# A two-layer hybrid attention and delta-rule backbone: high and low parts of queries, keys and values written by the stage that makes them, and loaded whole by the attention

## The chip, the cores and the metric

The kernel runs on one core of one Trainium2 chip. The metric is the device time of a run in microseconds (us). The profile covers one execution; its span goes from the first to the last instruction of the program, and a run's time is somewhat longer than the span.

The engines in the rows are PE (TensorE matmuls; PEld are its weight loads), DVE (VectorE), ACT (ScalarE), POOL (GpSimd) and SP (SyncE, which here issues all the transfers, in its own order; SPq is its sequencer). Each engine works through its instructions in the order in which they stand. Transfers run on the core's 16 DMA engines.

## The reference, cut to what matters

There are two layers over 1024 latent and 256 context tokens of width 1024. Each layer projects its input once, and the result goes to a latent attention (8 heads, 96 numbers per query and key, 64 per value) and to a gated delta rule (4 heads of 128). Both results go through one output projection, and a squared-relu MLP follows.

```python
p = h @ w_in
q_a, kv_a, k_r, qkv, z, a, b = jnp.split(p, _split_points(IN_SIZES), axis=-1)
q = (rmsnorm(q_a, q_a_g) @ w_q_b).reshape(B, T, MLA_HEADS, MLA_QK_DIM)
kv = (rmsnorm(kv_a, kv_a_g) @ w_kv_b).reshape(B, T, MLA_HEADS, MLA_NOPE_DIM + MLA_V_DIM)
q_nope, q_pe = q[..., :MLA_NOPE_DIM], q[..., MLA_NOPE_DIM:]
k_nope, v = kv[..., :MLA_NOPE_DIM], kv[..., MLA_NOPE_DIM:]
...
s = jnp.einsum('bqhd,bkhd->bhqk', qi, k).astype(jnp.float32) * scale
p = jax.nn.softmax(s, axis=-1).astype(v.dtype)
return jnp.einsum('bhqk,bkhd->bqhd', p, v)
```

All is float32. The kernel multiplies a pair of float32 matrices as three products of float32r parts: a value is its high part (a cast to float32r) plus a low part (the value minus the high part), and `mm3` adds high by high, high by low and low by high.

## The kernel before, in words

Tokens lie in three blocks: block 0 holds the 256 context tokens, blocks 1 and 2 hold 512 latent tokens each. The last layer has no queries in block 0. A layer has three stages.

Stage 1 (`stage1`) makes the input projection by tiles of 128 output columns (PE rows `mm`), the short convolutions, gates and chunk preparation of the delta rule, and the projections of the attention. `kv_proj` works block by block: four products of 128 output rows (`kps`, keys of two heads each, 64 numbers a head) and then one product for each 128 tokens (`vps`, values of all heads). `q_proj` makes four such products of queries (`qps`) and two more with the rotary columns of all heads. Each result is copied by ACT from its PSUM bank to a staging tile (`staged`, L720; tag `stg`, 3 buffers) and written to memory: keys to `kd` (L736, a transfer of 2 heads x 64 rows x 256 or 512 tokens), values to `vd` (L742, 128 tokens x 8 heads x 64), queries to `qd` (L766, again 2 x 64 x tokens) and rotary queries to `qd` (L779, 8 heads x 16 rows x tokens; in blocks 1 and 2 from a tile `rq` that shares the staging tiles' tag). Rotary keys follow in `kpe` (L601). The products' banks have the tag `pj`, with two buffers. So a product waits for a bank, a bank for its copy, and a copy for a staging tile whose write has landed.

Stage 2 runs attention and delta rule side by side. A unit of attention is 256 queries of one head (one per head for block 0, two for blocks 1 and 2). `front` makes the scores (`St` and `S` on PE), takes them out with their maximum (DVE, L878) and applies the exponential (ACT, L896). `back` transposes the results (`pt`), splits them into parts (`ph` on ACT, L927; `pl` on DVE, L928) and multiplies by the values (`o`). A head's keys, values and a block's queries come through `parts`: a transfer of at most 512 numbers per partition to a tile `raw` (L831, 3 buffers), an ACT cast to the high part (L832), and a subtraction for the low part (L834, on POOL except for the first heads, where it is on DVE). Key tiles alternate between two places by the head's parity, value tiles and query tiles have two buffers.

Stage 3 is output projection, norm and MLP.

The order on each engine is not written by hand. A scheduler places the instructions when the program is built, from its own estimate of their times. PE, ACT, DVE, POOL and SP then keep that order on the chip. Transfers take eight semaphores in turn, so that a transfer is issued only when the eighth before it has landed.

Of the kernel before, what the change touches and what calls it, by code (L numbers as in the profile page):

```python
# [17 lines left out]
P = 128  # L18
# [55 lines left out]
def host_layout(inp):  # L74
# [16 lines left out]
    # tiles of output columns: q 4, k 4, v 4, misc, kv_a, q_a 2, z 4  # L91
# [4 lines left out]
    # the rotary columns: first halves of all heads, second halves of all heads  # L96
# [19 lines left out]
class K:  # L116
# [13 lines left out]
    # ---------------------------------------------------------------- set-up  # L130
# [51 lines left out]
            # features and weights are queued behind the modulation's weights  # L182
# [93 lines left out]
    def ada_sum(self, l, v, m):  # L276
        """Eight columns that came by way of Pool and ACT, from their halves and the bias."""
        to = self.mod[l][v][:, m:m + 8]
        self.nc.vector.tensor_tensor(to, self.part[:, 0, v], self.part[:, 1, v], op=ALU.add)
        self.nc.vector.tensor_tensor(to, to, self.bada[l][:, m:m + 8], op=ALU.add)  # L280

    def load_sc(self, sp):
        """silu(c) and silu(c_ctx) on all partitions."""
        self.sc_b = []
        for v in range(2):
            t = sp.tile([P, D], F32, name=f"scr{v}")
            self.nc.sync.dma_start(t, self.scd[v].partition_broadcast(P))
            self.sc_b.append(t)

    def gain(self, l, j, vs):  # L290
        """(1 + scale) * gain of norm j."""
# [45 lines left out]
    def norm_mod(self, xs, rb, b, l, which, pool):  # L337
        """Modulated RMSNorm of block b (8 tiles [128, n]) into the high and low parts of h."""
# [22 lines left out]
    # ---------------------------------------------------------------- stage 1  # L361
    def stage1(self, l, last):
        """Input projection, short conv, gates, chunk preparation, latent attention's projections."""
# [8 lines left out]
        # the solves may go on into the next stage  # L372
# [16 lines left out]
        self.kd = dtile("kd", [H_A, DQK, NT])  # L389
        self.qd = dtile("qd", [H_A, DQK, NT])  # L390
        self.vd = dtile("vd", [H_A, P, NTT, 64])
# [40 lines left out]
        def conv_tile(m, blocks, it=None):  # L432
            """Projection, short conv, twice the silu."""
# [63 lines left out]
        lr = el.enter_context(self.pool(f"lr_{l}", side=self.osd))  # L497

        def first():
            """The first two output tiles, side by side, while the norm goes on."""  # L500
# [72 lines left out]
    def kpe(self, l, it, sp, tpp):  # L573
        """Rotary key part of all heads, and the gate columns by token."""
# [8 lines left out]
        for b, n, ps in it:  # L583
# [31 lines left out]
    def gates(self, l, stp):  # L615
        """Per-token scalars of both directions, [128 tokens, direction, tile, head]."""
# [45 lines left out]
        # the squares are of twice the features  # L662
# [24 lines left out]
    # ---- latent attention's low-rank parts  # L687
# [6 lines left out]
    def lowrank(self, raw, b, g, sp, stp):  # L694
        """RMSNorm of the low-rank features of block b, as high and low parts."""
# [21 lines left out]
    def staged(self, sp, src, n):  # L717
        t = sp.tile([P, 512], F32, tag="stg", name="stg", bufs=3)
        with self.hp_():
            self.nc.scalar.copy(t[:, :n], src)  # L720
        return t

    def kv_proj(self, l, raw, sp, mmp, stp):
        """Keys (but for the rotary part) and values of all heads, to DRAM as high and low parts."""
# [4 lines left out]
        for b, (t0, n) in enumerate(BLOCKS):  # L729
            xh, xl = self.lowrank(raw, b, g, sp, stp)[0]  # L730
            for m in range(4):
# [3 lines left out]
                t = self.staged(sp, ps[:, :n], n)  # L735
                nc.sync.dma_start(self.kd[2 * m:2 * m + 2, 0:64, t0:t0 + n], t[:, :n])  # L736
            for o in range(0, n, P):
# [3 lines left out]
                e = self.staged(sp, ps, 512)  # L741
                nc.sync.dma_start(self.vd[:, :, t, :].rearrange("h p c -> p h c"),  # L742
                                  e.rearrange("p (h c) -> p h c", c=64))

    def q_proj(self, l, raw, sp, mmp, stp):
# [3 lines left out]
        # the scale of the scores  # L749
        nc.vector.tensor_scalar(g, g, SM_SCALE, None, op0=ALU.mult)  # L750
        wk = [self.wload(io["w_qb"][l, :, k * QB:(k + 1) * QB]) for k in range(2)]
        for b in sorted({b for b, _ in raw}):
# [10 lines left out]
            for m in range(4):  # L763
                ps = qmm(m)
                t = self.staged(sp, ps[:, :n], n)
                nc.sync.dma_start(self.qd[2 * m:2 * m + 2, 0:64, t0:t0 + n], t[:, :n])  # L766
# [3 lines left out]
            for m in range(2):  # L770
                if b:
                    t = sp.tile([P, 512], F32, tag="stg", name="rq1", bufs=3)
# [4 lines left out]
                else:  # L777
                    t = self.staged(sp, ps[m][:, :n], n)
                nc.sync.dma_start(self.qd[:, 64 + 16 * m:80 + 16 * m, t0:t0 + n], t[:, :n])  # L779
# [10 lines left out]
        # the first scores wait for the products before them, not for the last transposes' banks  # L790
# [26 lines left out]
    def attention(self, l, last, ap, psA, psO):  # L817
# [4 lines left out]
        def parts(hi, lo, src):  # L822
            """Loads [p, n] or [p, t, n] values as their high and low parts."""
            p, m = src.shape[0], src.shape[1]
            w = 1 if len(src.shape) == 2 else src.shape[2]
            for c in range(0, m, 512 // w):
                e = min(m, c + 512 // w)
                raw = ap1.tile([P, 512], F32, tag="raw", name="raw", bufs=3)[:p, :(e - c) * w]
                if w > 1:
                    raw = raw.rearrange("p (t n) -> p t n", n=w)  # L830
                nc.sync.dma_start(raw, src[:, c:e])  # L831
                nc.scalar.copy(hi[:, c:e], raw)  # L832
                eng = nc.gpsimd if len(cur) > 3 else nc.vector
                eng.tensor_tensor(lo[:, c:e], raw, hi[:, c:e].bitcast(F32), op=ALU.subtract)  # L834

        def load(h):
            t = {}
            for nm in ("kh", "kl"):
                t[nm] = (ap2 if h % 2 else ap1).tile([DQK, NT], F32R, tag=nm, name=nm)
            parts(t["kh"], t["kl"], self.kd[h])  # L840
# [651 lines left out]
```

## Time and profile before

| | |
|---|---|
| median of 3 runs | 3953.94 us (3952.34 to 3956.1) |
| span of the profiled execution | 3929.9 us |
| difference of the two | 24.0 us |
| PE busy | 3517.4 us, 90% of the span |
| DVE, POOL, ACT busy | 2134.2, 1516.0 and 1459.3 us |
| moved by transfers | 372.52 MB, mean 95 GB/s |

No time of its own is given for the profiled execution beyond its span; the 24.0 us lie around the span and are taken as unchanged. Stage 2 lies at about 565 to 1075 us in layer 0 and 2620 to 3085 us in layer 1. The key, value and query projections of stage 1 lie at 105 to 264 us and at 2228 to 2378 us. A row of the stretches gives, for each engine, busy us and the number of its instructions, then PEclk (the granted share of TensorE's clock), the mean busy share of the 16 DMA engines, and what they moved. A wait is put down to what ended last before the waiting instruction. A time in brackets in a timeline is idle time before that instruction.

### The profile page before, as it was taken

What the parts mean: (1) busy time and instruction counts of PE and PEld (TensorE: products, weight loads), DVE (VectorE), ACT (ScalarE), POOL (GpSimd) and SP (SyncE); (2) the same over time, 40 slices, a digit from 0 to 9 for tenths busy, and PEclk for the clock granted to TensorE, in tenths of its full rate; (3) what the DMA queues carried; (4) which work ended last, traced back from release to release, by engine and by line L of the source; (5) the groups of instructions that cost most, each with busy time, mean ns of one, the idle gap of its engine ahead of it and who ended that gap; (6) DMA issues with size and microseconds to landing.
All of it is one profiled execution on the core that took longest, in us unless ns stands there. A gap on an engine that the chain in (4) does not pass through costs nothing.

```text
span 3929.9 us, 52618 instructions
## 1 busy us (share of the span) xinstructions
PE 3517.4 (90%) x19001; PEld 2992.1 (76%) x19001; DVE 2134.2 (54%) x4080; ACT 1459.3 (37%) x3156; POOL 1516.0 (39%) x1358
## 2 busy tenths in 40 slices
PE   8789977887887898999999978888889899999998
PEld 4668766787776777888888757767788788888887
DVE  5157855565769995333333627776667533333334
ACT  4334355565633111121112524336666531222122
POOL 3124864433354232232223313675533352333232
PEclk8899987898998899999999979989899899999999
DMA  5343465535353352111111334454653511111111
GB/s 186 91 136 116 139 149 94 112 93 95 77 199 102 129 180 81 43 44 38 38 33 43 102 94 132 144 147 109 125 101 81 132 57 46 52 51 49 44 54 54
DMA packets 335892, 372.52 MB, mean 95 GB/s; under 512 B 126849, under 2 KB 226577, under 8 KB 333969
## 3 DMA queue, kind: packets, MB, share of 16 engines
q1 hardware_dynamic: 335632, 369.18, 34.3%
q8 instruction: 149, 2.44, 0.3%
q14 instruction: 111, 0.90, 0.1%
HBM read 280.65 MB, written 88.42 MB: 94 GB/s over the span
## 4 chain that ended last, share of the span: by engine, by line
PE 57%; DVE 13%; DMA 12%; issue 5%; ACT 4%; POOL 3%; SPq 1%; POOLq 0%; DVEq 0%; ACTq 0%
PE f2ps L313 6%; PE f2ps L314 6%; PE f2ps L315 6%; PE fps L314 6%; PE fps L315 6%; PE fps L313 6%; DVE adaj L272 3%; DMA raw<-kd 3%; PE g L984 3%; PE o L916 3%; PE pt L924 2%; DVE cacc L444 2%; DVE A L1427 2%; DMA rinv<-rinv 2%; DMA adaw<-w_adaT 1%
## 5 line engine op out<-in xcount | busy, mean ns | idle before, releaser
L308 POOL TENSOR_TENSOR wlo<-wraw,whi 128x1024 fp32r<-128x1024 f32 (+1 forms) x190 | 462.3, 2441 | 1217.8 <-ACT whi L307 1217.8
L1304 DVE SCALAR_TENSOR_TENSOR x<-f2ps,mod,x 128x512 f32<-128x512 f32 (+1 forms) x648 | 440.9, 689 | 353.3 <-PE f2ps L315 353.1
L307 ACT CAST whi<-wraw 128x1024 fp32r<-128x1024 f32 (+1 forms) x190 | 195.6, 1046 | 1008.0 <-PE f2ps L314 692.7
L313 PE MATMUL f2ps<-ah,whi 128*128 128x512 f32 (+1 forms) x1296 | 474.4, 371 | 31.4 <-DVE x L1304 27.2
L314 PE MATMUL f2ps<-al,whi 128*128 128x512 f32 (+1 forms) x1296 | 478.5, 370 | 0.8 <-DVE al L1293 0.8
L313 PE MATMUL fps<-hh,whi 128*128 128x512 f32 (+1 forms) x1288 | 471.3, 368 | 8.8 <-ACT hh L351 8.8
L315 PE MATMUL f2ps<-ah,wlo 128*128 128x512 f32 (+1 forms) x1296 | 477.4, 369 | 0.0
L314 PE MATMUL fps<-hl,whi 128*128 128x512 f32 (+1 forms) x1288 | 474.1, 368 | 0.0
L315 PE MATMUL fps<-hh,wlo 128*128 128x512 f32 (+1 forms) x1288 | 472.9, 368 | 0.0
L1293 DVE TENSOR_TENSOR al<-relu,ah 128x256 fp32r<-128x256 f32 (+1 forms) x161 | 111.5, 699 | 512.9 <-POOL relu L1292 512.9
L313 PE MATMUL mm<-hh,whi 128*128 128x512 f32 (+1 forms) x880 | 333.1, 380 | 35.0 <-ACT craw L430 22.1
L314 PE MATMUL mm<-hl,whi 128*128 128x512 f32 (+1 forms) x880 | 331.4, 377 | 3.6 <-DVE hl L352 2.1
L315 PE MATMUL mm<-hh,wlo 128*128 128x512 f32 (+1 forms) x880 | 327.6, 374 | 0.8 <-POOL wlo L308 0.8
L928 DVE TENSOR_TENSOR pl<-pt,ph 128x512 fp32r<-128x512 f32 x328 | 222.2, 686 | 194.7 <-ACT ph L927 182.1
L313 PEld LDWEIGHTS f2ps<-ah,whi 128*128 128x128 f32 x1296 | 248.2, 192 | 74.4 <-DVE x L1304 29.9
L313 PEld LDWEIGHTS fps<-hh,whi 128*128 128x128 f32 x1288 | 243.7, 190 | 49.1 <-ACT hh L351 9.1
L314 PEld LDWEIGHTS f2ps<-al,whi 128*128 128x128 f32 x1296 | 248.7, 192 | 40.7 <-DVE al L1293 1.0
L315 PEld LDWEIGHTS f2ps<-ah,wlo 128*128 128x128 f32 x1296 | 248.4, 192 | 40.1
L314 PEld LDWEIGHTS fps<-hl,whi 128*128 128x128 f32 x1288 | 244.0, 189 | 40.1 <-POOL hl L357 0.3
L315 PEld LDWEIGHTS fps<-hh,wlo 128*128 128x128 f32 x1288 | 243.9, 189 | 39.8
L924 PE MATMUL pt<-ctab,p 128*128 128x128 f32 x1312 | 219.9, 287 | 32.9 <-ACT p L896 12.7
L1292 POOL TENSOR_TENSOR relu<-relu 128x256 f32<-128x256 f32 (+1 forms) x161 | 159.5, 996 | 225.2 <-ACT ah L1291 209.7
(287 smaller groups left out, 7520.6 us busy)
## 6 DMA issues: line engine op xcount, KB each, us to landing
wraw<-w_ff SPq DMA_DIRECT2D x128, 512.0 KB
adaw<-w_adaT SPq DMA_DIRECT2D x160, 256.0 KB
wraw<-w_in SPq DMA_DIRECT2D x40, 512.0 KB
QK<-QK SPq DMA_DIRECT2D x72, 256.0 KB
A<-A SPq DMA_DIRECT2D x40, 256.0 KB
v<-vtd SPq DMA_DIRECT2D x40, 256.0 KB
kt<-ktd SPq DMA_DIRECT2D x40, 256.0 KB
kT<-kTd SPq DMA_DIRECT2D x36, 256.0 KB
```

Source lines behind the costliest of these rows:

```text
L272: nc.vector.tensor_tensor_reduce(out=j, in0=w, in1=self.sc_b[v][:, s], op0=ALU.mult, op1=ALU.add, scale=1.0, scalar=acc if i else self.bad ...
L307: nc.scalar.copy(hi[:, :n], raw[:, :n])
L308: nc.gpsimd.tensor_tensor(lo[:, :n], raw[:, :n], hi[:, :n].bitcast(F32), op=ALU.subtract)
L313: then(mm(ps, lhsT=lh, rhs=rh, start=start, stop=False))
L314: then(mm(ps, lhsT=lh, rhs=rl, start=False, stop=False))
L315: then(mm(ps, lhsT=ll, rhs=rh, start=False, stop=stop))
L916: nc.tensor.matmul(o, lhsT=v[:, k, :], rhs=x[:, j, :], start=k == 0 and i == 0, stop=k == nkt - 1 and i == 1)
L924: self.mark = nc.tensor.transpose(tp[:, j, i * P:(i + 1) * P], pp[i][:, (k0 + j) * P:(k0 + j + 1) * P], self.ident)
L928: nc.vector.tensor_tensor(pl, tp, ph.bitcast(F32), op=ALU.subtract)
L984: nc.tensor.matmul(ps[:, h, :], lhsT=lhs[:, h, :], rhs=rhs[:, h, :], start=True, stop=True)
L1292: nc.gpsimd.tensor_tensor(r[:, :n], r[:, :n], r[:, :n], op=ALU.mult)
L1304: nc.vector.scalar_tensor_tensor(xs, ps[:, :n], g2, xs, op0=ALU.mult, op1=ALU.add)
```

## The change

Memory now holds both parts. `kd`, `qd` and `vd` have twice their size: keys and queries with an axis for the part, values with high and low part side by side (128 numbers a head and token). In stage 1 `staged` casts a product's bank to the high part on ACT and subtracts on DVE for the low part, and each key and query tile is written by two transfers, the value tile by one with both parts. The staging tiles are now four, of both parts each; three of them lie in space that the solves of the delta rule use later. `kpe` and the rotary queries are split in the same way. In stage 2 `parts` is gone: a head's keys are one transfer (96 x 2 x 1280), its values one (128 x 1280), a block's queries one (96 x 2 x tokens, now three buffers), straight into the operands of the products.

```diff
-        self.kd = dtile("kd", [H_A, DQK, NT])
-        self.qd = dtile("qd", [H_A, DQK, NT])
-        self.vd = dtile("vd", [H_A, P, NTT, 64])
+        self.kd = dtile("kd", [H_A, 2, DQK, NT])
+        self.qd = dtile("qd", [H_A, 2, DQK, NT])
+        self.vd = dtile("vd", [H_A, P, NTT, P])
...
+            parts = [sp.tile([P, 512], F32R, tag=nm, name=nm) for nm in ("gm", "gl")]
             for r, o in ((R1, 64), (R2, 80)):
-                nc.sync.dma_start(self.kd[:, o:o + 16, t0:t0 + n].rearrange("h r n -> r h n"),
-                                  kp[r, :n].unsqueeze(1).to_broadcast([16, H_A, n]))
+                nc.scalar.copy(parts[0][r, :n], kp[r, :n])
+                nc.gpsimd.tensor_tensor(parts[1][r, :n], kp[r, :n], parts[0][r, :n].bitcast(F32), op=ALU.subtract)
+                for i, x in enumerate(parts):
+                    nc.sync.dma_start(self.kd[:, i, o:o + 16, t0:t0 + n].rearrange("h r n -> r h n"),
+                                      x[r, :n].bitcast(F32).unsqueeze(1).to_broadcast([16, H_A, n]))
...
+    def staged(self, src, view):
+        t = self.stg[self.nstg % 4]
+        self.nstg += 1
+        hi, lo = view(t)
         with self.hp_():
-            self.nc.scalar.copy(t[:, :n], src)
-        return t
+            self.nc.scalar.copy(hi, src)
+            self.nc.vector.tensor_tensor(lo, src, hi.bitcast(F32), op=ALU.subtract)
+        return t.bitcast(F32)
...
-                t = self.staged(sp, ps[:, :n], n)
-                nc.sync.dma_start(self.kd[2 * m:2 * m + 2, 0:64, t0:t0 + n], t[:, :n])
+                t = self.staged(ps[:, :n], lambda t: (t[:, :n], t[:, 512:512 + n]))
+                for i in range(2):
+                    nc.sync.dma_start(self.kd[2 * m:2 * m + 2, i, 0:64, t0:t0 + n], t[:, i * 512:i * 512 + n])
...
-        def parts(hi, lo, src):
-                nc.sync.dma_start(raw, src[:, c:e])
-                nc.scalar.copy(hi[:, c:e], raw)
-                eng = nc.gpsimd if len(cur) > 3 else nc.vector
-                eng.tensor_tensor(lo[:, c:e], raw, hi[:, c:e].bitcast(F32), op=ALU.subtract)
...
         def load(h):
+            k = (ap2 if h % 2 else ap1).tile([DQK, 2, NT], F32R, tag="k", name="k")
+            nc.sync.dma_start(k.bitcast(F32), self.kd[h].rearrange("s r n -> r s n"))
+            v = ap2.tile([P, NTT, P], F32R, tag="v", name="v", bufs=2)
+            nc.sync.dma_start(v.bitcast(F32), self.vd[h])
+            cur[h] = k, v
```

SP in stage 1 of layer 0, from the first key write of block 0 to the last value write of block 2, before:

```order
L736 DMA kd_507<-stg 2x64x256 x2
L742 DMA vd_509<-stg 128x8x64 x2
L736 DMA kd_507<-stg 2x64x512 x3
L305 DMA wraw<-w_in 128x1024
L736 DMA kd_507<-stg 2x64x512
L742 DMA vd_509<-stg 128x8x64 x4
L736 DMA kd_507<-stg 2x64x512 x4
L742 DMA vd_509<-stg 128x8x64 x4
```

and the same place after (L755 writes keys, L765 values):

```order
L755 DMA kd_507<-stg 2x64x256 x4
L765 DMA vd_509<-stg 128x8x128 x2
L755 DMA kd_507<-stg 2x64x512 x4
L305 DMA wraw<-w_in 128x1024
L755 DMA kd_507<-stg 2x64x512 x4
L765 DMA vd_509<-stg 128x8x128 x4
L755 DMA kd_507<-stg 2x64x512 x8
```

Each key write stands twice, with the same shape of 2 x 64 x tokens, and the weight load (`wraw`) stands among them as it did.

ACT in stage 2 of layer 0, where the third head's keys come in, before (`kh`, `qh`, `v` are high parts that it casts from `raw`):

```order
L927 CAST ph<-pt 128x512
L832 CAST qh<-raw 96x512
L832 CAST kh<-raw 96x512
L896 ACTIVATE p,sm<-p,mn 128x256 x2
L1014 COPY U_4377<-B_4367 32x4x32 x4
L927 CAST ph<-pt 128x512
```

SP at the same head's keys, after (L857 loads queries, L849 keys):

```order
L857 DMA q<-qd_508 96x2x512
L849 DMA k<-kd_507 96x2x1280
L1011 DMA A_4444<-A_0_0_2670 64x4x64
L1011 DMA A_4444<-A_1_0_2673 64x4x64
L857 DMA q<-qd_508 96x2x256
```

The casts from `raw` between the attention's own ACT work are gone, and the third head's keys are issued right behind the queries of the second head's last block, while two units of that head are still to come.

## Rows read from the trace of the kernel before

**Rows 1.** Stretches: the projections (keys and values, then queries) of both layers.
```profile
105.00:175.00 70.00, 45.37 (x212) 36.30 (x211) 6.66 (x14) 18.68 (x37) 7.33 (x6) 0.76 0.30 86
175.00:264.00 89.00, 76.31 (x394) 64.64 (x395) 30.87 (x32) 29.81 (x87) 18.13 (x10) 0.92 0.33 100
2228.00:2298.00 70.00, 43.95 (x189) 32.36 (x189) 7.02 (x13) 21.47 (x57) 6.62 (x5) 0.79 0.37 101
2298.00:2378.00 80.00, 66.81 (x310) 55.95 (x311) 30.50 (x29) 23.29 (x56) 19.66 (x10) 0.87 0.31 98
```
**Rows 2.** Stretches: stage 2 of layer 0 and of layer 1.
```profile
565.00:1075.00 510.00, 410.45 (x2845) 373.10 (x2845) 314.89 (x916) 302.55 (x741) 207.54 (x258) 0.88 0.49 99
...
2620.00:3085.00 465.00, 409.09 (x2929) 371.11 (x2928) 313.96 (x907) 306.30 (x730) 209.49 (x286) 0.91 0.49 106
```
**Rows 3.** Timeline, ACT and then PE, key and value products of layer 1.
```profile
2282.11 0.59 ACT L720 COPY stg<-kps 128x512 f32<-128x512 f32 x1 [5.32 <-DMA kd<-stg]
...
2282.75 0.80 PE L313 MATMUL vps<-whi,nh 128*128 128x512 f32 x1 [4.93 <-ACT stg L720]
```
**Rows 4.** Narrow stretches with writes outstanding: keys 512 wide, queries 256 wide.
```profile
2278.00:2289.00 11.00, 2.50 (x5) 1.59 (x6) 0.00 (x0) 1.17 (x2) 0.00 (x0) 0.68 0.13 51
...
186.00:189.00 3.00, 3.00 (x18) 2.59 (x17) 0.00 (x0) 0.37 (x1) 0.00 (x0) 1.00 0.14 48
```
**Rows 5.** SP's timeline beside the first of them.
```profile
2274.12 9.92 SPq L736 DMA_DIRECT2D kd<-stg  x4
```
**Rows 6.** Transfers of the page by line: count and KB of one.
```profile
vd<-stg SPq DMA_DIRECT2D x20, 256.0 KB
...
kd<-stg SPq DMA_DIRECT2D x16, 256.0 KB
qd<-stg SPq DMA_DIRECT2D x16, 256.0 KB
...
qd<-rq SPq DMA_DIRECT2D x8, 256.0 KB
...
kd<-stg SPq DMA_DIRECT2D x8, 128.0 KB
...
qd<-stg SPq DMA_DIRECT2D x6, 128.0 KB
```
**Rows 7.** Narrow stretches: rotary query writes, value writes, 512-byte pieces of `kTd`.
```profile
216.00:218.00 2.00, 0.00 (x0) 0.00 (x0) 0.26 (x1) 0.58 (x2) 1.38 (x1) 1.00 0.75 242
2274.00:2275.00 1.00, 1.00 (x4) 0.81 (x3) 0.00 (x0) 0.10 (x1) 0.00 (x0) 0.50 1.08 256
221.50:223.50 2.00, 2.00 (x7) 1.52 (x6) 0.00 (x0) 2.00 (x14) 0.03 (x1) 0.50 0.96 298
```
**Rows 8.** Groups by line: a DVE subtraction that reads a PSUM bank.
```profile
L928 DVE TENSOR_TENSOR pl<-pt,ph 128x512 fp32r<-128x512 f32 x151 | 102.4, 686 | 98.9 <-ACT ph L927 95.3 <-PE o L916 2.4 <-issue 0.3
```
**Rows 9.** Waits in stage 2, layer 0 and then layer 1: total us, times, longest.
```profile
ACT kh L832 <- DMA raw<-kd: 83.5, 18, 10.1
...
ACT kh L832 <- DMA raw<-kd: 53.9, 12, 9.3
```
**Rows 10.** Timeline of layer 0, ACT and then PE, one wait for keys.
```profile
701.23 0.62 ACT L832 CAST kh<-raw 96x512 fp32r<-96x512 f32 x1 [4.52 <-DMA raw<-kd]
...
703.14 1.97 PE L1036 MATMUL g<-X,A 128*128 128x64 f32 x8 [4.21 <-ACT X L1029]
```
**Rows 11.** Chain that ended last, by line, stage 2 of layer 0, then layer 1.
```profile
by line: DMA raw<-kd 16.9%; DMA rinv<-rinv 10.3%; PE g L984 10.2%; PE o L916 8.8%; PE pt L924 6.9%; issue 5.2%; DMA B<-B 5.0%; PE S L313 3.4%; PE S L314 3.2%; PE S L315 3.2%; ACT p L896 2.3%; DMA rb<-rinv 2.0%; DVE p L878 1.9%; DMA raw<-vd 
...
by line: PE g L984 14.6%; PE o L916 13.9%; PE pt L924 11.4%; DMA raw<-kd 8.4%; PE S L313 5.2%; PE S L315 5.0%; PE S L314 4.9%; issue 2.8%; DMA wraw<-w_out 2.6%; DVE pl L928 1.8%; DMA raw<-vd 1.8%; DMA rinv<-rinv 1.8%; ACT ph L927 1.7%; DVE 
```
**Rows 12.** Work on `raw` in stage 2 of both layers: DVE, ACT, POOL busy.
```profile
565.00:1075.00 510.00, 0.00 (x0) 27.79 (x54) 55.87 (x54) 0.88 0.49 99
...
2620.00:3085.00 465.00, 0.00 (x0) 24.23 (x47) 51.41 (x48) 0.91 0.49 106
```

More of the change, by code (lines that the diff above doesn't have):

```diff
@@ L497, in stage1 @@
         lr = el.enter_context(self.pool(f"lr_{l}", side=self.osd))
+        self.open_stage(sv, lr)
         def first():
@@ L715, in lowrank, with open_stage @@
         return res
-    def staged(self, sp, src, n):
-        t = sp.tile([P, 512], F32, tag="stg", name="stg", bufs=3)
+    def open_stage(self, sv, sp):
+        both = sv.tile([P, 2048], F32R, tag="both", name="stg")
+        blb = sv.tile([P, 1024], F32R, tag="blb", name="stg")
+        own = sp.tile([P, 1024], F32R, name="stg")
+        self.stg = [both[:, :1024], both[:, 1024:], blb, own]
+        self.nstg = 0
+    def staged(self, src, view):
+        t = self.stg[self.nstg % 4]
+        self.nstg += 1
+        hi, lo = view(t)
         with self.hp_():
-            self.nc.scalar.copy(t[:, :n], src)
-        return t
+            self.nc.scalar.copy(hi, src)
+            self.nc.vector.tensor_tensor(lo, src, hi.bitcast(F32), op=ALU.subtract)
+        return t.bitcast(F32)
     def kv_proj(self, l, raw, sp, mmp, stp):
@@ L740, in kv_proj, with heads @@
                 self.mm3(ps, xh[:, o:o + P], xl[:, o:o + P], wh[:, 512:], wl[:, 512:], True, True)
-                e = self.staged(sp, ps, 512)
-                nc.sync.dma_start(self.vd[:, :, t, :].rearrange("h p c -> p h c"),
-                                  e.rearrange("p (h c) -> p h c", c=64))
+                def heads(t):
+                    e = t.rearrange("p (h c) -> p h c", c=P)
+                    return e[:, :, 0:64], e[:, :, 64:]
+                e = self.staged(ps.rearrange("p (h c) -> p h c", c=64), heads)
+                nc.sync.dma_start(self.vd[:, :, t, :].rearrange("h p c -> p h c"), e.rearrange("p (h c) -> p h c", c=P))
     def q_proj(self, l, raw, sp, mmp, stp):
@@ L764, in q_proj @@
                 ps = qmm(m)
-                t = self.staged(sp, ps[:, :n], n)
-                nc.sync.dma_start(self.qd[2 * m:2 * m + 2, 0:64, t0:t0 + n], t[:, :n])
+                t = self.staged(ps[:, :n], lambda t: (t[:, :n], t[:, 512:512 + n]))
+                for i in range(2):
+                    nc.sync.dma_start(self.qd[2 * m:2 * m + 2, i, 0:64, t0:t0 + n], t[:, i * 512:i * 512 + n])
             if b:
@@ L771, in q_proj @@
                 if b:
-                    t = sp.tile([P, 512], F32, tag="stg", name="rq1", bufs=3)
+                    t = sp.tile([P, 512], F32, tag="rq1", name="rq1", bufs=1)
                     q2 = sp.tile([P, 512], F32, tag="ls", name="rq2", bufs=2)
@@ L777, in q_proj @@
                 else:
-                    t = self.staged(sp, ps[m][:, :n], n)
-                nc.sync.dma_start(self.qd[:, 64 + 16 * m:80 + 16 * m, t0:t0 + n], t[:, :n])
+                    t = ps[m][:, :n]
+                x = self.staged(t[:, :n], lambda t: (t[:, :n], t[:, 512:512 + n]))
+                for i in range(2):
+                    nc.sync.dma_start(self.qd[:, i, 64 + 16 * m:80 + 16 * m, t0:t0 + n], x[:, i * 512:i * 512 + n])
     def stage2(self, l, last):
@@ L820, in attention @@
         cur = {}
-        def parts(hi, lo, src):
[L824 to L830, printed above, removed]
-                nc.sync.dma_start(raw, src[:, c:e])
-                nc.scalar.copy(hi[:, c:e], raw)
-                eng = nc.gpsimd if len(cur) > 3 else nc.vector
-                eng.tensor_tensor(lo[:, c:e], raw, hi[:, c:e].bitcast(F32), op=ALU.subtract)
-        def load(h):
[L837 to L840, printed above, removed]
-            t["v"] = v = ap2.tile([P, NTT, P], F32R, tag="v", name="v", bufs=2)
-            parts(v[:, :, 0:64], v[:, :, 64:], self.vd[h])
-            cur[h] = t
+        def load(h):
+            k = (ap2 if h % 2 else ap1).tile([DQK, 2, NT], F32R, tag="k", name="k")
[3 more added lines that the diff above has]
+            cur[h] = k, v
         def loadq(h, b):
             t0, n = BLOCKS[b]
-            cur[h, b] = r = [ap1.tile([DQK, 512], F32R, tag=nm, name=nm, bufs=2) for nm in ("qh", "ql")]
-            parts(r[0][:, :n], r[1][:, :n], self.qd[h, :, t0:t0 + n])
+            cur[h, b] = q = ap1.tile([DQK, 2, 512], F32R, tag="q", name="q", bufs=3)
+            nc.sync.dma_start(q[:, :, :n].bitcast(F32), self.qd[h, :, :, t0:t0 + n].rearrange("s r n -> r s n"))
         state = {}
@@ L861, in front @@
                 load(h)
-            t = cur[h]
-            qh, ql = cur[h, b]
+            kk, v = cur[h]
+            qq = cur[h, b]
             nk = NCTX if b == 0 else NT
@@ L871, in scores @@
                 q = slice(half * 256 + i * P, half * 256 + (i + 1) * P)
-                self.mm3(s, qh[:, q], ql[:, q], t["kh"][:, c0:c1], t["kl"][:, c0:c1], True, True)
+                self.mm3(s, qq[:, 0, q], qq[:, 1, q], kk[:, 0, c0:c1], kk[:, 1, c0:c1], True, True)
             pp = [ap.tile([P, NT], F32, tag="p", name="p", bufs=4) for _ in range(2)]
@@ L904, in front @@
             nc.sync.dma_start(rb[0:64], rd.rearrange("i p -> (i p)").partition_broadcast(64))
-            state[h, b, half] = (pp, rb, nk // P, t["v"])
+            state[h, b, half] = (pp, rb, nk // P, v)
         def back(h, b, half):
```

## The prediction

> **What bounds the kernel now.** I read the stretches first, to find where PE has room. PE is busy 90% of the span, so a change can win only where PE idles or where its clock is low. Two places of this change are such. In stage 2 PE is busy 410 of 510 us in layer 0 and 409 of 465 in layer 1, at a granted clock of 0.88 and 0.91 [rows 2]: 100 and 56 us idle. In the projections of stage 1 it is busy 45 of 70 us and 44 of 70 while keys and values are made, and 76 of 89 and 67 of 80 while queries are made [rows 1].
>
> Then I asked what ends the waits there. In stage 2 the reader is to see ACT stand before a cast of keys until `raw` has landed: 83.5 us in 18 waits in layer 0, 53.9 in 12 in layer 1 [rows 9]. ACT keeps its order, so everything behind the cast waits too, and PE with it: 4.52 us on ACT become 4.21 on PE a little later [rows 10]. The chain of work that ended last runs through these transfers for 16.9% of 510 us and 8.4% of 465, that is 86 and 39 us, and for 1.8% of 465 (8 us) through those of the values [rows 11].
>
> In stage 1 the wait is another one. ACT stands before a copy to a staging tile until an earlier key write has landed, 5.32 us for one, and PE then stands 4.93 us for ACT [rows 3]. Why a write takes so long is seen in the narrow stretch: four key writes are issued within 9.92 us [rows 5], and from 2278 to 2289 us, with nothing but these outstanding, the 16 DMA engines are busy to 0.13 and move 51 GB/s [rows 4]. 0.13 of 16 is two engines. A write of 2 heads x 64 rows goes through two engines, and the next one goes through the same two, otherwise the share would rise while several are outstanding. A 256 KB write thus costs 262144 B / 51 GB/s = 5.1 us of that pair, a 128 KB one 131072 / 48 = 2.7 us [rows 4]. The key phase is bound by this pair: per layer 8 x 5.1 + 4 x 2.7 = 52 us of its 70.
>
> **The change part by part.** The sum is made against the profiled execution: a span of 3929.9 us, and 24.0 us around it to the median of 3953.94.
>
> *Key and query writes, doubled.* Both layers have 16 + 8 key writes and 16 + 6 query writes from the staging tile [rows 6]; two of the six are rotary and are counted below. That is 32 of 256 KB and 12 of 128 KB: 32 x 5.1 + 12 x 2.7 = 196 us of the pair's time. After the change each stands twice with the same shape, so 196 us are added.
>
> *Rotary queries, doubled.* Ten more writes, eight of 256 KB [rows 6]. They move 242 GB/s, not 51 [rows 7], 1.1 us each: 10 us.
>
> *Value writes.* Twenty of 256 KB become twenty of 512 KB, in pieces of 512 bytes, not 256. At 256 bytes they move 256 GB/s, and other 512-byte pieces 298 [rows 7]: 1.76 - 1.02 = 0.74 us each, 15 us. The Trainium skill (DMA: Bandwidth & Descriptors, Specifications) speaks for this part: line rate needs pieces of at least 512 bytes, and shorter ones are read, modified and written. By it these bytes would be nearly free, and the sum 15 us smaller; the row, at 256 GB/s with short pieces, does not show such a loss, and I keep the 15.
>
> So 221 us of transfer time are added to phases of 309 us in all [rows 1]. How much room is there? In each phase the pair carries the narrow writes and a sixteenth of all else, which I estimate at 298 GB/s [rows 7]. Layer 0, keys: 86 GB/s x 70 us = 6.0 MB, less 2.6 MB narrow, 3.4 MB, 11 us; with 52 that is 63 of 70. In the same way 73 of 89 (layer 0, queries), 67 of 70 and 60 of 80. Free are 7 + 16 + 3 + 20 = 46 us. With all of it used the phases grow by 221 - 46 = 175 us; with none by 221. Below that, PE can run ahead of the pair by four staging tiles of 2 x 5.1 us, 41 us a layer, if its order holds enough other products and their weights are there: 175 - 82 = 93. I take 170, near the first value, because the weight loads stand in SP's order among the writes, as before, and so cannot run ahead.
>
> *The subtractions.* DVE gets one per staged tile, 24 for keys, 20 for values and 30 for queries, 0.69 us each as one that reads a bank [rows 8]: 51 us over both layers. The eight rotary tiles that POOL finished now pass ACT as well, 0.59 us each. DVE is busy 7 of 70 and 31 of 89 us there [rows 1], and the waits for the pair hide all of it. Without that cover each would hold a bank or a tile 0.7 to 1.3 us longer, 56 us at most.
>
> *Rotary keys.* Per block two casts and two subtractions more, on ACT and POOL, ahead of the writes. Nothing like it is in the trace; the nearest is one staged copy of 0.59 us [rows 3] plus 0.69 [rows 8], twice per block, 6 blocks: 15 us if all lies on the path, 0 if none. Their writes wait in SP's order with the weights behind them. I take 5.
>
> *Stage 2.* Gone are 52 us of ACT and 107 of POOL [rows 12], all beside PE's work and worth nothing by themselves, and the waits for `raw`. What is late next is the softmax chain: DVE waits 95.3 us for `ph` in layer 0 [rows 8], and a part of these waits is itself ACT standing at a cast. The gain cannot be more than what the chain spends in these transfers, 86 + 39 + 8 = 133 us, nor can it exceed the idle 156. It is not less than nothing by much: the bytes of the three loads double (about 10 MB a layer against 99 GB/s x 510 us = 50 MB [rows 2]) and delay the small transfers behind them, but they land directly. PE now waits for keys itself, and all of PE's order is queued behind that; yet the third head's keys are issued two units before their use. Two units of 40 in 510 us are 25 us, more than any wait of [rows 9], 10.1. I take 85, some two thirds of the chain's share, because the waits for `ph` and for the scores stay; ends 23 (half of the keys' 125 us stays, as waits of PE: 85 - 62) and 133.
>
> The sum: +170 + 5 - 85 = +90. 3929.9 + 90 = 4020 of span, **4044 us** with the 24 around it.
>
> **The rivals.** *A. The forecast:* the pair of engines decides, 4044.
>
> *B. Stage 2 wins, faster than before.* The mechanism is the backlog of staging tiles: PE's other products cover 41 us of writes in each layer, stage 1 costs 93, and the chain of stage 2 shortens by its whole 133. Time 3954 + 93 + 5 - 133 = 3919. It decides from the point at which the stretches of the projections grow by less than stage 2 shrinks. For it: PE is fully busy for the 3 us in which 256-wide writes are outstanding [rows 4], and its clock in stage 2 has 10% to regain [rows 2]. Against it: PE idles a third of the key phase already [rows 1], so the covering work is used up before.
>
> *C. The second part goes through other engines.* Then the pair carries no more than before, the rotary and value writes and the rotary keys cost 10 + 15 + 5 at most, and the time is 3954 + 30 - 85 = 3899. Against it: with several writes outstanding the share stays at 0.13 [rows 4, 5]. The Trainium skill (DMA: Bandwidth & Descriptors, Why a DMA increments its semaphore by 16 and not by 1) gives a rule that speaks against this change: a transfer takes the largest number of engines up to 16 that divides its slowest dimension larger than one, and the lowest-numbered ones. By that rule both parts, with 2 as that dimension, meet on one pair, and the trace agrees at 0.13 of 16; C is then out.
>
> *D. The change doesn't do what it says: stage 2 still waits, now on PE.* A head's keys are one transfer of 960 KB; the first scores need all of it, and SP's order can hold it back behind waits of others. With half of the keys' waits left the gain is 23, and the time 3954 + 170 + 5 - 23 = 4106. For it: the smaller transfers were late by up to 10.1 us [rows 9]. Against it: they were issued when a `raw` tile came free, and that reason is gone.
>
> **How the numbers follow.** Chances: A 0.68, B 0.10, C 0.04, D 0.18. A's own ends, 93 + 5 - 85 and 221 + 15 - 23, give +13 to +213, 3967 to 4167. Left out below 3955 are B and C (0.14), above 4135 the upper ends of A and D (0.06), where no room is used and little is gained; so the range is 3955 to 4135. A difference of 0.2%, 8 us, is about what a measurement of this kernel can tell from no change. Faster by more: B and C, 0.13. Within: 0.04, the edges of A and B. Slower by more: 0.83.
>
> **What would show it.** Stage 1 first: the stretch from the first key product to the last query product should take some 240 us in each layer, against 159 and 150 [rows 1], with long times at a DMA share of 0.13 and 51 GB/s, and ACT waiting for `kd<-stg` some 10 us at a time where it was 5 [rows 3]. If the share is 0.26 there, C is right. If these stretches grow by under 50 us a layer, the cover of B is there. In stage 2 the chain should hold no loads of keys, and PE's idle time should fall from 156 us to about 90; if PE waits for `k` or `q` for more than some 40 us in all, D is right. The forecast is wrong if the two-engine writes turn out to be hidden, or if stage 2 gives back more than 133 us, which only a regained clock could do.

## The result, and the profile after

The changed kernel takes 4131.98 us (median of 4 runs, 4126.7 to 4142.01), the kernel before 3953.14 us (4 runs, 3948.79 to 3956.1): a ratio of 1.0451, with a 95% interval of 1.0432 to 1.0471. It is 179 us slower. The prediction had 4044, and a range that ends at 4135, 3 us above the measured median.

The span and the busy times from the page of the changed kernel:

```profile
span 4140.2 us, 52501 instructions
...
PE 3522.0 (85%) x19001; PEld 2993.1 (72%) x19001; DVE 2161.8 (52%) x4140; ACT 1417.1 (34%) x3056; POOL 1421.3 (34%) x1264
```

PE does the same products in nearly the same time (3517 us before, 3522 after) and idles 618 us where it idled 412. Where it does is seen in the stretches. For each layer I cut the trace at PE's own instructions: the first key product, the last query product, the first scores (the start of stage 2) and the first output product after stage 2. The rows of before, cut like this (they take the place of [rows 1, 2], whose cuts were read by eye), layer 0 and then layer 1; columns as there, duration, busy us of PE, PEld, DVE, ACT and POOL, granted clock, DMA share, GB/s:

```profile
106.50:247.50 141.00, 111.46 (x548) 92.03 (x548) 34.08 (x41) 44.57 (x118) 19.24 (x12) 0.85 0.32 95
247.50:512.60 265.10, 239.95 (x1290) 201.93 (x1290) 199.36 (x217) 96.25 (x256) 173.26 (x133) 0.95 0.46 136
512.60:1098.80 586.20, 462.56 (x3177) 417.42 (x3176) 351.54 (x1021) 347.63 (x843) 245.91 (x322) 0.87 0.50 102
...
2226.60:2355.10 128.50, 99.19 (x449) 78.61 (x449) 27.34 (x35) 41.96 (x108) 18.63 (x11) 0.84 0.34 97
2355.10:2612.30 257.20, 226.03 (x1132) 185.54 (x1132) 193.94 (x217) 93.76 (x249) 159.89 (x121) 0.95 0.45 134
2612.30:3117.60 505.30, 428.27 (x3010) 385.81 (x3009) 330.71 (x936) 322.36 (x756) 232.07 (x307) 0.90 0.50 107
```

The same six of the changed kernel:

```profile
104.60:331.70 227.10, 128.70 (x605) 104.24 (x605) 63.57 (x85) 48.51 (x124) 21.45 (x13) 0.74 0.30 94
331.70:638.60 306.90, 236.23 (x1234) 197.20 (x1233) 189.39 (x208) 96.07 (x251) 181.08 (x148) 0.88 0.47 131
638.60:1199.20 560.60, 450.17 (x3178) 407.02 (x3177) 345.97 (x1020) 322.75 (x788) 186.11 (x259) 0.89 0.58 123
2323.50:2515.70 192.20, 108.45 (x449) 84.36 (x449) 45.70 (x68) 43.24 (x110) 18.61 (x11) 0.72 0.30 98
2515.70:2798.70 283.00, 227.65 (x1133) 185.74 (x1132) 195.21 (x213) 95.67 (x250) 169.10 (x132) 0.92 0.49 138
2798.70:3327.40 528.70, 423.41 (x3010) 384.03 (x3009) 332.36 (x937) 300.79 (x709) 179.35 (x255) 0.88 0.62 121
```

The projections grow by 86 and 64 us. The rest of stage 1, between the last query product and the first scores, grows by 42 and 26; stage 1 as a whole grows by 217. Stage 2 shrinks by 26 in layer 0 and grows by 23 in layer 1. Everything else together is 5 us shorter: 217 - 2 - 5 = 210 between the two spans. The medians differ by 179, because the profiled execution of before was a quick one (a span of 3929.9 us, where seven runs beside the experiments with the writes and the row sums have 3945.8 to 3960.9, each about 2 us under its time) and that of the changed kernel the slowest of its four. Single stretches therefore carry some 20 us of spread.

**Stage 1: the pair of engines, and SP behind it.** The stretch that answers to [rows 4], in which SP issues nothing but two-engine writes until 210 us, then ACT's timeline, SP's and DVE's in and beside it:

```profile
184.00:214.00 30.00, 4.40 (x10) 2.15 (x9) 1.50 (x4) 1.82 (x4) 0.00 (x0) 0.55 0.13 51
```

```profile
197.96 0.59 ACT L737 CAST stg<-vps 128x512 fp32r<-128x512 f32 x1 [14.60 <-DMA kd<-stg]
```

```profile
180.25 29.98 SPq L755 DMA_DIRECT2D kd<-stg  x7
```

```profile
183.39 0.69 DVE L738 TENSOR_TENSOR stg<-kps,stg 128x512 fp32r<-128x512 f32 x1 [0.59 <-ACT stg L737]
```

DMA share and rate are the 0.13 and 51 GB/s of [rows 4], now for 30 us on end, in which PE works 4.4. ACT's wait for an earlier key write is 14.60 us where [rows 3] had 5.32. New is the third row: SP needs 29.98 us to issue seven writes, 4.3 us each, near the 5.1 that the pair needs by the prediction to carry one. It does not stand for data: the last part of these key tiles is made by 184.1 us (fourth row). The list of instructions on the key tensor shows the same (count, then shortest, median and longest issue in ns; the first row is of the kernel before, the second of the changed one):

```profile
L736 SPq DMA_DIRECT2D kd<-stg x24: 478/498/2362, 107.5 to 2282.7; - x24
```

```profile
L755 SPq DMA_DIRECT2D kd<-stg x48: 492/2817/7162, 105.6 to 2430.0; - x48
```

While the pair is behind, issuing itself takes a median of 2.8 us instead of 0.5, and what stands between these writes in SP's order is issued late: the value writes, which spread over the engines [rows 7], take a median of 3.3 us to issue instead of 0.45. That is why the part after the projections grew too. SP's timeline at the last query product of layer 0, the waits from 320 to 420 us (total, times, longest), and the first 28.3 us behind that product as a stretch:

```profile
332.65 11.05 SPq L789 DMA_DIRECT2D qd<-stg  x3
343.80 4.91 SPq L305 DMA_DIRECT2D wraw<-w_in  x1
```

```profile
ACT whi L307 <- DMA wraw<-w_in: 26.2, 1, 26.2
PE tp L474 <- DVE cacc L451: 25.8, 1, 25.8
```

```profile
331.70:360.00 28.30, 3.15 (x14) 2.25 (x12) 2.05 (x4) 2.10 (x4) 0.00 (x0) 0.60 0.25 83
```

A load of weights is issued only at 343.8 us, behind the query writes, and takes 4.9 us to issue. ACT stands 26.2 us until it has landed, the rest of ACT's order stands behind that, and PE is busy for 3 of 28 us; in the kernel before PE was busy for 20.5 of the 28.3 us behind its last query product. Layer 1 has the same wait at its last query product, 35.4 us.

**Stage 2: the waits for keys are gone, the time is not.** No engine that computes has a wait that is put down to `k` or `q` (SP has, 4.0 us at the longest, and layer 1's chain has three pieces of them, 18 us together); the casts on ACT and their waits of [rows 9] don't exist any more. In their place stand waits for the reciprocal row sums, which in both kernels go to memory and come back to all partitions (`rinv` written, `rb` read). SP's and POOL's waits for them, of the changed kernel, layer 0 and then layer 1:

```profile
SPq L913 <- DMA rinv<-rinv: 197.3, 30, 13.1
...
POOL ob L950 <- DMA rb<-rinv: 78.5, 10, 15.5
...
SPq L913 <- DMA rinv<-rinv: 199.4, 27, 13.2
...
POOL ob L950 <- DMA rb<-rinv: 117.8, 14, 16.2
```

The same waits in the kernel before, layer 0 and then layer 1:

```profile
SPq L904 <- DMA rinv<-rinv: 137.9, 25, 8.3
...
POOL ob L941 <- DMA rb<-rinv: 16.6, 4, 6.3
...
SPq L904 <- DMA rinv<-rinv: 139.5, 23, 9.1
...
POOL ob L941 <- DMA rb<-rinv: 7.8, 2, 6.8
```

SP stands before the read back until the write has landed, for 277 us of stage 2 before and 397 after. The chain of layer 1 holds the same write for 16.0% where [rows 11] had 1.8% (of the changed kernel the chain does not reach back to layer 0):

```profile
by line: DMA rinv<-rinv 16.0%; PE g L993 9.9%; PE o L925 8.0%; PE pt L933 6.3%; DMA B<-B 5.8%; issue 4.3%; PE S L313 2.9%; PE S L315 2.7%; PE S L314 2.6%; DVE U L1025 2.6%; DMA craw<-catg 2.5%; DMA wraw<-w_out 2.2%; DMA rb<-rinv 2.2%; DMA q
```

### The profile page after: what moved, and what is told of

It is laid out like the page before. It is cut to its first block, busy times and chain, and to the rows that moved or that the text cites. A ratio compares the mean times of both kernels' runs of the same rounds, so it can differ in the third digit from the quotient of the medians.

```text
span 4140.2 us, 52501 instructions
## 1 busy us (share of the span) xinstructions
PE 3522.0 (85%) x19001; PEld 2993.1 (72%) x19001; DVE 2161.8 (52%) x4140; ACT 1417.1 (34%) x3056; POOL 1421.3 (34%) x1264
## 5 line engine op out<-in xcount | busy, mean ns | idle before, releaser
L313 PEld LDWEIGHTS mm<-hh,whi 128*128 128x128 f32 x880 | 175.3, 199 | 96.8 <-ACT craw L431 51.2
```

Source lines behind the costliest of these rows:

```text
L313: then(mm(ps, lhsT=lh, rhs=rh, start=start, stop=False))
```

## The experiments

The theory after the two traces: stage 1 is set by the pair and by SP standing behind it; stage 2 by the round trip of the row sums. The rivals: in stage 1 the subtractions, casts and bytes; in stage 2 the doubled loads. Two edits take away one suspect each, in both kernels.

**Writes by head (`w_after`, `w_before`).** The diff in the changed kernel, for keys; queries likewise, and the kernel before without the part dimension:

```diff
-for i in range(2):
-    nc.sync.dma_start(self.kd[2 * m:2 * m + 2, i, 0:64, t0:t0 + n], t[:, i * 512:i * 512 + n])
+for j in range(2):
+    nc.sync.dma_start(self.kd[2 * m + j, :, 0:64, t0:t0 + n].rearrange("s r n -> r s n"),
+                      t.rearrange("p (s c) -> p s c", s=2)[64 * j:64 * j + 64, :, :n])
```

> Each staged key or query tile of the changed kernel is written by head (two transfers of 64 rows x 2 parts x n) in place of by part (two of 2 heads x 64 rows x n): same bytes, same number of transfers. Theory (two engines carry all the narrow writes and set the length of the projections): with a write spread over the engines the stretch from first key product to last query product falls from 227 and 192 us to 120 or below in both layers, the DMA share of 0.13 with 51 GB/s is gone, and the time is some 3860 (3820 to 3950), below the kernel before. Rival (the added subtractions and casts, or the doubled bytes, are what costs): the stretches stay above 190 us and the time above 4050.

> The kernel before, each staged key or query write split into its two heads (64 rows x n each), so that the rows and not the heads are the outermost dimension; same bytes, twice the number of these transfers. Theory (the pair of engines already binds the projections before the change): the stretches of 141 and 128 us fall to 110 and 100, the time to some 3893 (3870 to 3920). Rival (PE's own work sets these stretches before, the pair only the changed kernel's): within 10 us of 3953.

**Row sums without memory (`r_after`, `r_before`).** The same in both kernels; `r` holds the reciprocal sums of 2 x 128 queries, one column each:

```diff
-rd = self.dr.tile([2, P], F32, name=f"rinv{l}_{h}_{b}_{half}")
-nc.sync.dma_start(rd.rearrange("i p -> p i"), r)
-rb = ap2.tile([P, 256], F32, tag="rb", name="rb", bufs=1)
-nc.sync.dma_start(rb[0:64], rd.rearrange("i p -> (i p)").partition_broadcast(64))
...
-nc.gpsimd.tensor_tensor(ob[0:64], ob[0:64], rb[0:64], op=ALU.mult)
+rb = psA.tile([P, 512], F32, tag="a", name="rbp")
+for i in range(2):
+    nc.tensor.matmul(rb[0:64, i * P:(i + 1) * P], lhsT=r[:, i:i + 1].to_broadcast([P, 64]), rhs=self.ident,
+                     start=True, stop=True)
+nc.vector.tensor_tensor(ob[0:64], ob[0:64], rb[0:64, :256], op=ALU.mult)
```

> The changed kernel, the reciprocal row sums no longer written to memory and read back to all partitions, but spread by two small matrix products (128 x 64 ones pattern, 128 columns) into a bank, with the last product on DVE in place of POOL. Theory (in stage 2 these round trips through memory, late under the doubled loads, have taken the place of the waits for the raw keys): stage 2 falls from 561 and 529 us by some 40 each, the time to some 4040 (4010 to 4070). Rival (the doubled loads slow stage 2 in another way, through the keys and queries that PE waits for): less than 30 us gained.

> The kernel before, with the same replacement of the round trip of the reciprocal row sums. Theory (before the change the loads of keys set stage 2 and the round trips a smaller part, some 60 us of the chain in layer 0 and 8 in layer 1): 20 to 60 us faster, some 3913. Rival (the round trips are covered by other work and matter in neither kernel): within 10 us of 3953.

Times beside 3953.85 us of the kernel before (7 runs), with the stretches of each profile, both layers added (projections; from there to the first scores; stage 2). The two kernels with both edits, which come next, stand here too, beside 3954.07 (7 runs):

| kernel | us | ratio to before, 95% | projections | to scores | stage 2 |
|---|---|---|---|---|---|
| before | 3953.14 | 1 | 270 | 522 | 1091 |
| after | 4131.98 | 1.0432 to 1.0471 | 419 | 590 | 1089 |
| `w_before` | 3869.43 | 0.9764 to 0.9806 | 203 | 510 | 1113 |
| `w_after` | 3888.54 | 0.9807 to 0.9869 | 230 | 532 | 1080 |
| `r_before` | 3795.87 | 0.9576 to 0.9618 | 271 | 527 | 952 |
| `r_after` | 3977.48 | 1.0039 to 1.0076 | 425 | 585 | 925 |
| `wr_before` | 3703.96 | 0.9355 to 0.9383 | 201 | 509 | 956 |
| `wr_after` | 3736.10 | 0.9436 to 0.9464 | 233 | 531 | 933 |

The writes by head take 243 us off the changed kernel and 84 off the kernel before, and 179 us between the two become 19. The theory's 3860 (up to 3950) holds for the changed kernel, though its layer 0 stays at 124 us, not 120 or below; the 3893 (3870 to 3920) for the kernel before was just too high. Both rivals, above 4050 and within 10 us of 3953, are out. Layer 0 of `w_after`, projections, and the issue of its key writes:

```profile
106.40:230.20 123.80, 114.00 (x605) 94.45 (x605) 64.58 (x85) 48.50 (x124) 21.02 (x13) 0.97 0.68 194
```

```profile
L755 SPq DMA_DIRECT2D kd<-stg x48: 574/612/1712, 107.9 to 2243.0; - x48
```

As many transfers of the same bytes, at a DMA share of 0.68 instead of 0.30, a granted clock of 0.97 instead of 0.74, and an issue of 0.61 us instead of 2.82. The order of the rows decided, not the number of transfers or bytes. By the Trainium skill (DMA: Bandwidth & Descriptors, Why a DMA increments its semaphore by 16 and not by 1) the outermost dimension, 64 rows here instead of 2 heads, divides among 16 engines instead of two; the trace agrees, with a share of 0.68 in place of 0.30.

The row sums take 154 us off the changed kernel (I expected 90) and 158 off the kernel before, where I expected 40. That the round trip binds both kernels alike, I had not seen. Waits of ACT for the raw keys in `r_before`, layer 0 and then layer 1:

```profile
ACT kh L832 <- DMA raw<-kd: 4.8, 5, 2.5
...
ACT kh L832 <- DMA raw<-kd: 14.3, 10, 4.2
```

In the stretches cut as above these were 83.5 and 56.5 us before. The loads of keys are untouched here, in the same pieces, into the same tiles, through the same casts, and 140 us of waiting for them have become 19. The waits which the prediction laid to the loads go with the round trip. By which way they go isn't shown: the edit ends SP's stand and also takes the last product off POOL, which in the kernel before stood idle ahead of that product for 107 and 41 us and which also makes the low parts that free the `raw` tiles. The stretch of stage 2, layer 0, `r_before` and then `r_after`:

```profile
513.20:1010.40 497.20, 462.37 (x3338) 404.79 (x3337) 371.45 (x1060) 348.79 (x844) 219.06 (x284) 0.98 0.41 115
```

```profile
640.90:1125.20 484.30, 461.82 (x3337) 405.49 (x3336) 361.73 (x1059) 322.33 (x786) 156.47 (x215) 0.98 0.49 136
```

PE is nearly the bound in both, 35 and 22 us idle, where it idled 124 and 110 with the round trip; 13 us are what direct loads save in this layer.

**Both edits (`wr_before`, `wr_after`), and who waits for the round trip (`q_before`).** `q_before` changes one word in two lines:

```diff
-nc.sync.dma_start(rd.rearrange("i p -> p i"), r)
+nc.gpsimd.dma_start(rd.rearrange("i p -> p i"), r)
...
-nc.sync.dma_start(rb[0:64], rd.rearrange("i p -> (i p)").partition_broadcast(64))
+nc.gpsimd.dma_start(rb[0:64], rd.rearrange("i p -> (i p)").partition_broadcast(64))
```

> The kernel before with both edits: writes by head, and the reciprocal row sums spread by matrix products. Theory (the pair of engines binds the projections, the round trips bind stage 2, in different stretches, so the two gains add: 84 and 158 us): 3712 (3695 to 3730). Rival (what one edit sets free the other wait takes up): 3740 or more.

> The changed kernel with both edits. Theory (with the pair and the round trips gone the change itself is left: by the stretches of the single edits some 49 us more from the first key product to the first scores, 27 to 33 us less in stage 2): 3733 (3715 to 3750), that is 10 to 30 us above the kernel before with both edits. Rival (the direct loads of the high and low parts pay once nothing else binds stage 2, as the prediction had it): at least 30 us below the kernel before with both edits.

> The kernel before, the write of the reciprocal row sums and its read back issued by POOL in place of SP; everything else as it was. SP stood 137.9 and 139.5 us in the two stretches of stage 2 until that write had landed, with the loads of keys behind it. Theory (the waits for the raw keys, 83.5 and 56.5 us, come from that stand of SP): ACT waits for raw for less than 40 us in both stretches together, and the time falls by 60 to 130 us, to some 3850. Rival (the loads of keys are late by themselves, or the round trip's own length decides): the waits for raw stay above 90 us, or they go and the products that wait for the row sums take their place; the time is within 30 us of 3953.

The two gains add: 84 + 158 = 242, measured 250. `wr_before`, at 0.9369, beats both kernels; it is the version to keep. The change itself, with nothing else in its way, costs 32 us there: 54 more in stage 1, 23 less in stage 2. I had expected 10 to 30; the rival, at least 30 us below, is out.

`q_before` takes 3975.04 us (ratio 1.0033 to 1.0066), slightly slower. Its waits in layer 0 (POOL, ACT, SP):

```profile
POOL rb L904 <- DMA rinv<-rinv: 128.3, 23, 8.9
...
ACT kh L832 <- DMA raw<-kd: 77.2, 15, 10.9
```

```profile
SPq L942 <- POOL ob L941: 98.1, 28, 13.5
```

The theory missed: ACT still waits for `raw` for 77 us in layer 0 and 50 in layer 1, where I expected less than 40 in all, and the time is the rival's. In layer 0 the stand moved to POOL at nearly its old size (128.3 of 137.9 us; in layer 1, 75.2 of 139.5), and POOL makes the low parts which free the raw tiles, and the products for which SP now waits. So the run does not tell whether the stand of the issuing engine or the trip's length is the cause. It says that this change of the issuing engine doesn't help, and how long the trip's write is (KB, then median us from issue to landing):

```profile
rinv<-rinv POOLq DMA_DIRECT2D x72, 1.0 KB, 9.3
```

**What stage 1 pays (`x2_before`, `wx2_before`, `w_nosub`).** `x2_before` adds the doubled writes to the kernel before and nothing else; `wx2_before` does the same with writes by head; `w_nosub` is `w_after` without the subtraction, its staging tiles set to zero once, so that it leaves out the low parts:

```diff
 nc.sync.dma_start(self.kd[2 * m:2 * m + 2, 0:64, t0:t0 + n], t[:, :n])
+nc.sync.dma_start(self.kx[2 * m:2 * m + 2, 0:64, t0:t0 + n], t[:, :n])
...
-self.nc.vector.tensor_tensor(lo, src, hi.bitcast(F32), op=ALU.subtract)
```

> The kernel before with one thing added: each staged key and query tile is written a second time, in the same shape (2 heads x 64 rows x n), to a scratch that nothing reads. This is the doubling of the narrow writes alone, without subtractions, wider tiles or other loads. Theory (the pair of engines is the mis-sized term: 196 us of its time, little room, and everything behind the last query product waits for its backlog too): the two stretches from the first key product to the first scores grow by 180 to 230 us together, stage 2 stays, the time is some 4150. Rival (a good part of the changed kernel's loss is in the rest of the change): they grow by less than 150 us.

> The kernel before with writes by head, and each of them again to a scratch that nothing reads. With the writes by head the change still costs 49 us from the first key product to the first scores (762 us against 712), of which leaving out the subtractions took 2 (760). Theory (the bytes, and twice as many transfers in SP's order, cost it): these stretches come to 740 or more, the time to some 3905. Rival (the cost is in the staging, the casts of the rotary parts and the wider tiles): within 12 us of 712, the time within 12 us of 3869.

> The changed kernel with writes by head, and the subtractions that make the low parts in the staging tiles left out (the tiles are set to zero once; values and keys and queries without rotary part then have zeros or old data as low parts). Its stretches from the first key product to the last query product were 124 and 106 us with them, 106 and 97 in the kernel before with writes by head. Theory (the subtractions hold banks and staging tiles longer): these stretches fall to 112 and 100 or below. Rival (the doubled bytes cost it): within 5 us of 124 and 106.

`x2_before` takes 4110.46 us beside 3925.22 of the kernel before (7 runs beside this one and `wx2_before`), 185 us more and a ratio of 1.0472, 1.045 to 1.0494: the doubled narrow writes alone cost what the whole change costs. Its four stretches of stage 1:

```profile
105.80:331.30 225.50, 125.10 (x549) 101.49 (x549) 34.31 (x41) 42.36 (x103) 19.23 (x12) 0.74 0.24 77
331.30:615.60 284.30, 242.55 (x1290) 203.26 (x1289) 201.41 (x219) 98.66 (x270) 176.20 (x138) 0.92 0.45 133
2319.00:2521.50 202.50, 107.96 (x449) 84.76 (x450) 27.39 (x35) 42.63 (x108) 18.62 (x11) 0.71 0.26 80
2521.50:2790.10 268.60, 226.42 (x1132) 186.48 (x1131) 196.35 (x217) 93.69 (x248) 160.19 (x121) 0.92 0.44 132
```

They sum to 981 us against 792: 158 more in the projections, 31 after them, 189 in all, as the theory had it (180 to 230), and stage 2 stays (1081 against 1091). The theory's time, some 4150, was reckoned from 3953, where 185 us more make 4138.

`wx2_before` is at 0.9814 (0.979 to 0.9838), `w_before` at 0.9785 (0.9764 to 0.9806): the same within their intervals. Its stretches of stage 1 come to 724 us against 712, at the edge of what the rival allowed (within 12) and below the theory's 740; the 12 us are no more than the spread of a stretch (the profiled execution took 3866.44 us, the median is 3849.97). Spread over the engines, the second copy of keys and queries costs 12 us at most by this pair. `w_nosub`, at 3885.47 us (2 runs), equals `w_after`; its stretches come to 760 against 762, so with writes by head the subtractions are hidden and the theory that they hold banks is out. Of the 49 us that the change costs in stage 1 with writes by head (762 against 712), at most some 12 are bytes of keys and queries; the rest (values of twice the size, rotary parts, four wider staging tiles in place of three) I did not take apart.

## Why the prediction was right, and what it mis-sized

Direction and mechanism held: the pair of engines decides. That the time lies in the range is luck, by 3 us: the measured change, 179 us, is twice the forecast 90. What happened is close to the case that the prediction left above 4135 with a chance of 0.06, no room used and little gained, which its own bounds put at 4167 at most: stage 1 as a whole found almost no room, and stage 2 gave back little. The forecast was 88 us low, by two terms of the sum, 42 us in stage 1 and up to 83 in stage 2; that they add up to more is because the two profiles lie 210 us apart and the medians 179.

*Stage 1: +175 forecast with the rotary keys, +217 measured.* The price of the pair's work was right: 196 us forecast for the doubled key and query writes, 189 measured alone in `x2_before`. The 30 us for rotary and value writes and rotary keys compare with 217 - 189 = 28. The step that failed is the free room of 46 us taken off. The projections did use some of it (158 of 196), but the prediction counted only up to the last query product. The backlog is then still there, SP has not issued the weights that follow, and 31 us come back (68 in the changed kernel). The other end, "with none by 221", was the right one. I had the hint: I wrote that the weight loads stand in SP's order among the writes, and used it only against PE's running ahead.

*The subtractions* at nothing: right with writes by head, 2 us by `w_nosub`; beside the pair's backlog they were not taken out.

*Stage 2: -85 forecast, -2 measured*, and -33, -27 and -23 in the pairs of kernels with one or both edits. The -2 and the -33 are one within the spread: profiles with the stage 2 of before lie between 1081 and 1113 us (`before`, `w_before`, `x2_before`, `wx2_before`), those with the stage 2 of the change at 1080 and 1089 (`w_after`, `after`). By every pair the gain was less than half of the 85. The mis-sized step is the chain's 86 + 39 us of `raw` taken as the worth of those loads. The chain names the transfer that came last, not what made it late. In [rows 11] the row sums' write stands right behind, at 10.3%, and I gave it no term. `r_before` shows that the waits for `raw` go with it: without the round trip stage 2 is 139 us shorter before the change and 164 after, and direct loads save 27. SP's stand for the write grew from 277 to 397 us; that the doubled bytes of the loads made it grow (DMA share 0.58 and 0.62 where it was 0.50) is argued, not shown. My lower end for the gain in stage 2, 23 us, came near, but for another reason.

*The time around the span.* The 24 us around the span are about 2. This shifts nothing in the sum, as it was used as a difference to the median.

*Rivals.* B (3919): the backlog had no cover; the stretches grew by 86 and 64 us, over its 50. C (3899): the share stayed 0.13, so the second part met the first on the pair; C's distribution is what `w_after` makes, and it gives 3889. D (4106) came nearest in time, and one half of it was right: stage 2 goes on waiting. But its reason was not: no wait of PE is put down to the head's keys of 960 KB.

*The signs.* Long times at 0.13 and 51 GB/s: there. ACT waiting some 10 us: 14.60 in the row shown, and 4.5 to 14.6 with a median of 9.4 in the seven such waits between 150 and 232 us. Projections "some 240 us": they grew by 86 and 64 from 141 and 129, in my eye's cuts of 159 and 150 some 245 and 214. PE's idle in stage 2 falling to about 90: wrong; over the whole stretches it went from 201 to 216 us.

## What to carry to other kernels

Price a doubled transfer by the engines that carry it, and by how much time these have left, not by the mean of all 16: here writes with 2 outermost ran at a share of 0.13. Put the long dimension outermost before adding bytes. A backlog in the engines did not end here with the phase that made it: the issuing queue stood too, so price what comes next in its order. A wait for a load that the chain names need not be worth its length: here 140 us of such waits became 19 with the loads untouched, so look also at what else stands in the order of the engine that issues them.

## What was not expected of the hardware

Issuing is not free of what is outstanding: SP needed a median of 498 ns to issue a two-engine write of keys before, 2817 ns (up to 7162) with twice as many, and 612 ns for as many transfers of the same bytes over more engines. The Trainium skill (DMA: Bandwidth & Descriptors, Issuing engines are not separate DMA queues) calls the time to initiate a transfer usually small beside the transfer; here it grew to 4.3 us a write in the stretch shown, near the 5.1 that 256 KB take at 51 GB/s.

A write of 1 KB in 256 pieces of 4 bytes took a median of 9.3 us from issue to landing in `q_before`, issued from POOL and beside other transfers, and taking out 72 of them with their reads was worth 158 us of 3954. With two small products and a multiplication in the place of each, PE had some 160 instructions more in stage 2 of layer 0 (x3338 in `r_before` against x3177) and the same 462 us of busy time, at a granted clock of 0.98 where it was 0.87.
